# Expert results scattered by token into zeroed DRAM rows and read back by plain transfers, in a mixture-of-experts tail

## The chip, the cores and the metric

The kernel runs on one core of one Trainium2 chip, as one program. The metric is the device time of an execution in microseconds. Before the change it was 1543.15 us, the median of three runs (1536.94, 1543.15 and 1543.61).

## The reference

Two blocks stand behind each other on 512 tokens of width 1024. The first (gated linear attention, a state-space layer and a feed-forward net) and the attention and convolution of the second come before the change; the change is in the second block's mixture of experts. Cut to what matters:

```
def hierarchical_moe(h, ...):                  # t: (512, 1024), 4 groups of 8 experts, D_EXPERT 128
    g_val, g_idx = top_k(softmax(t @ rg_w + rg_b), 1)
    e_val, e_idx = top_k(softmax(logits of the chosen group), 2)     # two experts a token
    combine = one_hot(group) * g_val * w_group
    out += einsum('tef,efd->td', silu(t @ e_gate) * (t @ e_up) * combine, e_down)
x = x + gt2 * hierarchical_moe(...)
return rmsnorm_2(x, final_norm_g)
```

Each token goes to two experts, so 1024 expert rows of 1024 numbers have to come back to 512 tokens and be added to `x`, before the norm over each row that ends the kernel.

## The kernel before

The expert stage handles the 32 experts two at a time, in 16 steps (j = 0 to 15, called expert steps here). A step has 128 slots, 64 for each of its experts; about 64 of the 128 are filled, as 1024 rows go to 16 steps. `route` and `slots` make, for each slot, the number of the token that it holds (`idx` for the gathers, `tok` for one-hot matrices), past the bound where the slot is empty.

A step does this. `expert_rows` (L1763), an indirect gather issued by POOL, brings the tokens' rows from `h_dram` to SBUF, three steps ahead. `expert_in` transposes them on PE (L1774) and evacuates them half on ACT, half on DVE (`xT`). `expert_up` multiplies with the gate and up weights (L1793), and ACT and DVE form the activation (L1795 to L1797). `expert_turn` transposes it (L1804), `expert_down` multiplies with the down weights (L1816), and DVE scales the rows by the combine weight (L1817) into `y`, one of three buffers (`ys`; in the trace `ey` and the two halves of a `wd` tile). SP loads the weights, 3 MB a step, into six slots (`wslots`), and each load waits until PE has done with the slot.

Steps 0 to 13 (`SPREAD` is 14) store `y` to `y_dram` from SP, 128 rows at the place j*128 (`down`, L2337). Steps 14 and 15 go another way: `split_rows` halves the f32 rows into two parts that PE multiplies with one-hot matrices (`spread_mm`, L1839), and `spread_add` (L1845) adds the sums from PSUM to `x2`, the residual in SBUF. After step 13's store, `gather_back` (L1861) runs eight indirect gathers on POOL, two for each of the four tiles of 128 tokens, that add rows of `y_dram` to `x2` while they land; `route_back` made their row numbers. `final_out` then norms each of the four tiles (ACT sum of squares L1874, POOL L1876, DVE L125 to L129 and L1881, ACT L1882) and stores it (L1884).

The program's order is not the written one: a list scheduler with a simulated timeline sets it, and `issue_after` and `behind` put single instructions behind others. Each engine then works its own list off in order, so an instruction that waits holds up all behind it on its engine; a transfer's issue is such an instruction on SP or POOL. In that list the weight loads stand behind `e.last_load`, which `down` set to its store.

Earlier, the feed-forward net of the first block runs beside `ada_part` (L855), which loads `ada_w_2` in 48 pieces of 512 KB from POOL (L862) for DVE to sum (L866).

Of the kernel before, what the change touches and what calls it, by code (L numbers as in the profile page):

```python
# [20 lines left out]
SEQ = 512  # L21
# [1671 lines left out]

def route_back(e, pool, T):

    V = e.nc.vector
    first, past = T("r0", 2, 4), T("rp", 2, 4)
    V.tensor_mul(e.scr, e.ohf, e.efirst[:, None, None, :].to_broadcast([128, 2, 4, 32]))
    V.reduce_sum(first, e.scr, axis=mybir.AxisListType.X)
    V.tensor_scalar(past, e.rank, 64.0, OUT, op0=OP.is_ge, op1=OP.mult)  # L1700
    V.tensor_add(past, past, e.rank)
    V.tensor_add(first, first, past)
    e.back = pool.tile([128, 2, 4], I32, name="back")
    V.tensor_copy(e.back, first)


def slot_sums(e, oh, place):
# [10 lines left out]
def slots(e, pool, oh, rnd=None):  # L1718

    V = e.nc.vector  # L1720
    rk = e.rank
    if rnd is not None:
        rk = pool.tile([128, 2, 4], F32, name="srk")
        V.scalar_tensor_tensor(rk, rnd.to_broadcast([128, 8]).rearrange("p (a t) -> p a t", a=2), -64.0, e.rank,
                               op0=OP.mult, op1=OP.add)
    V.tensor_tensor(oh, rk.rearrange("p a t -> p (a t)")[:, :, None].to_broadcast([128, 8, 64]),
                    e.cnt[:, None, :].to_broadcast([128, 8, 64]), op=OP.is_equal)
    p = slot_sums(e, oh, e.place16).rearrange("p (x v) -> p x v", v=2)
    idx = pool.tile([128, 16], I32, name="sidx")
    col = pool.tile([128, 16], F32, name="scol")  # L1730
    V.tensor_copy(col, p[:, :, 0])
    add = lambda out, c: V.scalar_tensor_tensor(out, col, float(c), p[:, :, 1], op0=OP.add, op1=OP.add)
    add(idx, 2 * SEQ)
    tok = pool.tile([128, 16, 4], F32, name="stok")
    for t in range(4):
        last = add(tok[:, :, t], 2 * SEQ - 128 * t)
    e.slots = [last] if rnd is not None else [last, e.placed]
    return idx, tok
# [84 lines left out]
def split_rows(e, y, hl, oh, tok):  # L1823
# [5 lines left out]
    for c in HALVES:  # L1829
        nc.scalar.copy(hl[0][:, c], y[:, c])  # L1830
        V.tensor_sub(hl[1][:, c], y[:, c], hl[0][:, c].bitcast(F32))

# [22 lines left out]

def gather_back(e):

    last = ()
    for t, a in ((0, 0), (1, 0), (2, 0), (0, 1), (3, 0), (1, 1), (2, 1), (3, 1)):
        with behind(e, last):  # L1860
            last = [e.nc.gpsimd.indirect_dma_start(  # L1861
                out=e.x2[:, t], out_offset=None, in_=e.y_dram,
                in_offset=bass.IndirectOffsetOnAxis(ap=e.back[:, a, t:t + 1], axis=0),
                bounds_check=SPREAD * 128 - 1, oob_is_err=False, compute_op=OP.add)]

# [76 lines left out]
def block(ctx, tc, A, out, stop=None, dbg=None):  # L1942
# [44 lines left out]
    for a in range(2):  # L1987
        nc.gpsimd.iota(e.tid[:, 4 * a:4 * a + 4, 1], pattern=[[128, 4]], base=-2 * SEQ, channel_multiplier=0,
                       allow_small_or_imprecise_dtypes=True)
    e.cnt = c.tile([128, 64], F32, name="cnt")  # L1990
    nc.gpsimd.iota(e.cnt, pattern=[[1, 64]], base=0, channel_multiplier=0, allow_small_or_imprecise_dtypes=True)
    e.m2c = c.tile([128, 8], F32, name="m2c")
    e.sh2c = c.tile([128, 8], F32, name="sh2c")
    e.h3_dram = dram("h3_dram", [SEQ, DM])
    e.y_dram = dram("y_dram", [SPREAD * 128, DM])
    e.hg = c.tile([128, 8], F32, name="hg")
# [146 lines left out]
    with P(name="f1", bufs=1, **Lf) as fp:  # L2143
# [4 lines left out]
        V.tensor_scalar(e.ca, e.ca, 0.5, None, op0=OP.mult)  # L2148

        def ada():  # L2150
            for i in range(6):
                yield from ada_part(e, fp, i)

# [111 lines left out]
    T = carve(c[:, 0], c[:, 1])  # L2265
    e.efirst = kp.tile([128, 32], F32, name="efirst")
    nc.gpsimd.iota(e.efirst, pattern=[[64, 32]], base=0, channel_multiplier=0, allow_small_or_imprecise_dtypes=True)
    rnd = kp.tile([128, 1], F32, name="rnd")
# [53 lines left out]
    with P(name="mo", bufs=1, **Lf) as mp:  # L2322
# [4 lines left out]
        def split(j):  # L2327
            split_rows(e, ys[j % 3], hl[j % 2], ohs[j % 2], tok0[:, j])

        def down(j):  # L2330
# [3 lines left out]
            if late and j > 10:  # L2334
                split(j)
            elif not late:
                e.last_load = nc.sync.dma_start(e.y_dram[j * 128:j * 128 + 128], y)  # L2337

        pieces = [p for j in range(n, 16) for p in expert_pieces(e, j, wslots[j % n])]
        early = pieces.pop(2)  # L2340
# [10 lines left out]
        for j in range(17):  # L2351
            if j - 2 in groups:
                spread(e, hl, ohs)
            if j == BACK + 1:
                gather_back(e)
            if 0 < j < 15:
# [5 lines left out]
            if j == 15:  # L2362
                down(j - 1)
                spread14(range(EARLY14))
            if j < 16:
                up = expert_up(e, j, xT[j % 2], wslots[j % n][0])
            if j == 0:
                with behind(e, (up,)):
                    expert_in(e, xT[1], xgs[1])
                route_back(e, kp, T)  # L2370
                nc.sync.dma_start(*early)
# [7 lines left out]
            if j == 11:  # L2379
# [8 lines left out]
                for i in range(SPREAD, 11):  # L2388
                    split(i)
    with P(name="co", bufs=1, **Lf) as cp:  # L2390
        nc.scalar.activation(cp.tile([128, 1], F32, name="warm"), e.eps, AF.Sqrt)
# [127 lines left out]
```

## Time and profile before

| | us |
|---|---|
| median of three runs | 1543.15 (1536.94 to 1543.61) |
| the profiled execution | 1536.67 |
| its span | 1534.9 |
| PE busy | 1449.8 (94%) |
| DVE busy | 886.0 (58%) |
| ACT busy | 656.2 (43%) |
| POOL busy | 534.2 (35%) |

The span runs from the first to the last instruction that the profiler saw, and the execution's time is 1.8 us longer. A busy share is a mean over all stages. What a change in the last stage is worth is read there: in the windows from 1380 us on, in the chain that ended last, and in the rows of the engines whose work it moves.

### The profile page before, as it was taken

Reading aid. Unit: us, or ns where it says so; the run is one execution under the profiler, and the core shown is the slowest. Engines: PE = TensorE matmul, PEld = TensorE weight load, DVE = VectorE, ACT = ScalarE, POOL = GpSimd, SP = SyncE. Lnnn points to the kernel's source line nnn. Section 1 sums busy time; section 2 is a strip of 40 time slices with the busy share of each in tenths; the row PEclk is TensorE's granted clock in tenths of the full one; section 3 lists DMA queues with packets and bytes.
Section 4 is the critical chain, followed back from the end, with each engine's and each line's share of the span. In section 5 each row is a group of like instructions: output and inputs, shape, how many; then the busy total and the mean of one; then the engine's idle time right before and its main releaser. Section 6 shows DMA issues by size and latency. Waiting matters only on the chain. (4 is left out here: it accounts for less than half of the span.)

```text
span 1534.9 us, 23800 instructions
## 1 busy us (share of the span) xinstructions
PE 1449.8 (94%) x9408; PEld 1230.7 (80%) x9408; DVE 886.0 (58%) x1532; ACT 656.2 (43%) x1081; POOL 534.2 (35%) x594
## 2 busy tenths in 40 slices
PE   7999999899999999999999999899999999988994
PEld 7999998677888899897997979898777777975542
DVE  6586644445244566645536454855788776544544
ACT  6564332645322333323223133447767773443323
POOL 0356888222001121412213022508777714112104
PEclk9999999999999999999999999899999999988997
DMA  5842222458463352554545343411221336868997
GB/s 208 190 92 97 90 87 100 115 168 263 150 230 107 114 192 83 192 193 163 194 137 176 125 166 138 144 64 52 93 72 63 106 119 221 344 267 293 411 406 177
DMA packets 73947, 253.49 MB, mean 165 GB/s; under 512 B 20912, under 2 KB 25792, under 8 KB 57188
## 3 DMA queue, kind: packets, MB, share of 16 engines
q1 hardware_dynamic: 38256, 180.18, 32.8%
q0 software_dynamic: 16192, 49.54, 11.6%
q10 hardware_dynamic: 19380, 22.17, 4.5%
q8 instruction: 76, 1.25, 0.3%
q14 instruction: 43, 0.35, 0.1%
HBM read 226.65 MB, written 32.17 MB: 169 GB/s over the span
## 5 line engine op out<-in xcount | busy, mean ns | idle before, releaser
L74 DVE TENSOR_TENSOR wlo<-raw,whi 128x2048 fp32r<-128x2048 f32 x73 | 177.7, 2434 | 125.0 <-ACT whi L73 125.0
L73 ACT CAST whi<-raw 128x2048 fp32r<-128x2048 f32 x76 | 145.2, 1911 | 184.2 <-PE ps L98 94.5
L1117 POOL TENSOR_TENSOR uc<-uc,u 128x512 f32<-128x512 f32 x77 | 114.7, 1490 | 75.7 <-ACT u L1114 69.2
L98 PE MATMUL ps<-wlo,hh 128*128 128x256 f32 x416 | 117.1, 283 | 2.5 <-DVE wlo L74 2.5
L97 PE MATMUL ps<-xhi,whi 128*128 128x264 f32 (+1 forms) x352 | 119.0, 340 | 0.0
L98 PE MATMUL ps<-xlo,whi 128*128 128x264 f32 (+1 forms) x352 | 117.9, 335 | 0.3 <-DVE xlo L1930 0.3
L99 PE MATMUL ps<-xhi,wlo 128*128 128x264 f32 (+1 forms) x352 | 117.5, 334 | 0.0
L97 PE MATMUL ps<-whi,hh 128*128 128x256 f32 x416 | 116.8, 283 | 0.0
L99 PE MATMUL ps<-whi,hl 128*128 128x256 f32 x416 | 116.5, 281 | 0.0
L99 PE MATMUL ps<-hn,wlo 128*128 128x512 f32 (+1 forms) x256 | 97.6, 382 | 0.0
L98 PE MATMUL ps<-hn,whi 128*128 128x512 f32 (+1 forms) x256 | 97.6, 382 | 0.0
L97 PE MATMUL ps<-hn,whi 128*128 128x512 f32 (+1 forms) x256 | 97.5, 383 | 0.0
L905 POOL TENSOR_TENSOR fr<-fr 128x512 f32<-128x512 f32 x32 | 52.6, 1643 | 110.7 <-ACT fr L904 110.4
L866 DVE SCALAR_TENSOR_TENSOR aacc<-araw,ca,aacc 128x1024 f32<-128x1024 f32 x42 | 55.7, 1326 | 46.3 <-DMA araw<-in_ada_w_dram 46.0
L98 PEld LDWEIGHTS ps<-wlo,hh 128*128 128x128 f32 x416 | 79.1, 190 | 3.7 <-DVE wlo L74 2.7
L97 PEld LDWEIGHTS ps<-whi,hh 128*128 128x128 f32 x416 | 78.9, 190 | 1.9 <-issue 1.7
L99 PEld LDWEIGHTS ps<-whi,hl 128*128 128x128 f32 x416 | 79.4, 191 | 0.0
L862 POOL DMA_DIRECT2D araw<-in_ada_w_dram x48 | 26.3, 548 | 145.3 <-DVE aacc L866 91.0
L97 PE MATMUL ps<-whi,xhi 128*128 128x256 f32 x256 | 74.9, 293 | 0.0
L99 PE MATMUL ps<-whi,xlo 128*128 128x256 f32 x256 | 74.3, 290 | 0.0
L98 PE MATMUL ps<-wlo,xhi 128*128 128x256 f32 x256 | 73.6, 287 | 0.0
L97 PEld LDWEIGHTS ps<-xhi,whi 128*128 128x128 f32 x352 | 65.9, 188 | 8.9 <-issue 2.2
(675 smaller groups left out, 4214.3 us busy)
## 6 DMA issues: line engine op xcount, KB each, us to landing
raw<-in_w_ff_dram SPq DMA_DIRECT2D x32, 1024.0 KB
wg<-in_w_eg_dram SPq DMA_DIRECT2D x26, 1024.0 KB
araw<-in_ada_w_dram POOLq DMA_DIRECT2D x48, 512.0 KB, 4.6
wd<-in_w_ed_dram SPq DMA_DIRECT2D x10, 1024.0 KB
raw<-in_w_glu_dram SPq DMA_DIRECT2D x8, 1024.0 KB
wse<-in_w_eg_dram SPq DMA_DIRECT2D x6, 1024.0 KB
y_dram<-wd SPq DMA_DIRECT2D x9, 512.0 KB
U<-u_dram POOLq DMA_DIRECT2D x16, 264.0 KB, 3.7
```

What stands on the lines that cost most here:

```text
L73: nc.scalar.copy(hi[:, :n], raw[:, :n])
L74: sub.tensor_sub(lo[:, :n], raw[:, :n], hi[:, :n])
L97: nc.tensor.matmul(out, lhsT=ah, rhs=bh, start=(first and i == 0), stop=False)
L98: nc.tensor.matmul(out, lhsT=ah, rhs=bl, start=False, stop=False)
L99: nc.tensor.matmul(out, lhsT=al, rhs=bh, start=False, stop=(last and i == n - 1))
L862: nc.gpsimd.dma_start(raw, A["ada_w_2"][k * 128:(k + 1) * 128, i * DM:(i + 1) * DM])
L866: V.scalar_tensor_tensor(acc, raw, e.ca[:, k:k + 1], acc, op0=OP.mult, op1=OP.add)
L905: nc.gpsimd.tensor_mul(r, r, r)
L1117: nc.gpsimd.tensor_add(y, y, tmp)
```

## The change

The results of steps 0 to 13 are no longer stored by slot. `slots` also makes `e.to`, for each slot the row a*512 + token, where a is 0 or 1 for a token's first or second expert (the one-hot sums carry 128 more for the second, from `e.tid`; `second` splits it off again), and past the bound where the slot is empty. `down` scatters `y` by these numbers into `y_dram`, now 1024 rows, with an indirect transfer issued by POOL. Rows whose expert is in steps 14 and 15 stay zero: four transfers of zeros from POOL, 1 MB each, fill the tensor during the feed-forward net. After step 13, `rows_back` loads the eight blocks of 128 rows with plain transfers from SP into weight slots that are free by then (slot 5 and half of slot 0; in the trace they bear names like `wg` and `wd`). DVE adds four of them to `x2` (tokens 0 to 255), POOL three, DVE the last one. `route_back` and `gather_back` go. `e.last_load` is no longer set in `down`.

```diff
 def slots(e, pool, oh, rnd=None):
-    V.tensor_copy(col, p[:, :, 0])
+    second = pool.tile([128, 16], F32, name="ssec")
+    V.tensor_scalar(second, p[:, :, 0], 127.5, -128.0, op0=OP.is_ge, op1=OP.mult)
+    V.tensor_add(col, p[:, :, 0], second)
...
+    if rnd is None:
+        V.scalar_tensor_tensor(second, second, -4.0, col, op0=OP.mult, op1=OP.add)
+        e.to = pool.tile([128, 16], I32, name="sto")
+        V.scalar_tensor_tensor(e.to, second, float(2 * SEQ), p[:, :, 1], op0=OP.add, op1=OP.add)
...
-def gather_back(e):
-
-    last = ()
-    for t, a in ((0, 0), (1, 0), (2, 0), (0, 1), (3, 0), (1, 1), (2, 1), (3, 1)):
-        with behind(e, last):
-            last = [e.nc.gpsimd.indirect_dma_start(
-                out=e.x2[:, t], out_offset=None, in_=e.y_dram,
-                in_offset=bass.IndirectOffsetOnAxis(ap=e.back[:, a, t:t + 1], axis=0),
-                bounds_check=SPREAD * 128 - 1, oob_is_err=False, compute_op=OP.add)]
+def rows_back(e, views):
+
+    for t in range(4):
+        for a in range(2):
+            e.nc.sync.dma_start(views[2 * t + a], e.y_dram[a * SEQ + t * 128:a * SEQ + t * 128 + 128])
...
+    V.tensor_scalar(e.tid[:, 4:8, 0], e.tid[:, 4:8, 0], 128.0, None, op0=OP.add)
...
-    e.y_dram = dram("y_dram", [SPREAD * 128, DM])
+    e.y_dram = dram("y_dram", [2 * SEQ, DM])
...
+        zero = fp.tile([128, DM], F32, name="zero")
+        nc.gpsimd.memset(zero, 0.0)
         def ada():
             for i in range(6):
+                if i < 4:
+                    nc.gpsimd.dma_start(e.y_dram[256 * i:256 * i + 256].rearrange("(p r) d -> p r d", r=2),
+                                        zero[:, None, :].to_broadcast([128, 2, DM]))
                 yield from ada_part(e, fp, i)
...
         def down(j):
             if late and j > 10:
-                split(j)
+                e.halves = split(j)
             elif not late:
-                e.last_load = nc.sync.dma_start(e.y_dram[j * 128:j * 128 + 128], y)
+                nc.gpsimd.indirect_dma_start(out=e.y_dram, out_offset=bass.IndirectOffsetOnAxis(ap=e.to[:, j:j + 1], axis=0),
+                                             in_=y, in_offset=None, bounds_check=2 * SEQ - 1, oob_is_err=False)
...
             if j == BACK + 1:
-                gather_back(e)
+                rows_back(e, yb)
...
             if j == 15:
                 down(j - 1)
+                with behind(e, (e.halves,)):
+                    for t in range(2):
+                        for a in range(2):
+                            V.tensor_add(e.x2[:, t], e.x2[:, t], yb[2 * t + a])
+                for y in (4, 5, 6):
+                    nc.gpsimd.tensor_add(e.x2[:, y // 2], e.x2[:, y // 2], yb[y])
                 spread14(range(EARLY14))
...
+        with behind(e, (e.halves,)):
+            V.tensor_add(e.x2[:, 3], e.x2[:, 3], yb[7])
```

What this does to POOL's list. In the rows, `h` is the buffer of an expert gather and `sidx` its row numbers; `x2t` is the residual `x2`; `sto` is `e.to`. A wait on `DMASW` with a number is for the landing of an earlier transfer issued by POOL (their semaphores are taken in turn, 0 to 7), one on `PE` or `DVE` for that engine. Before, the last four expert gathers are followed by the gathers back:

```order
L1763 DMA h_12545<-h_dram,sidx 128x1024 [waits DMASW4_49,PE_49]
L1763 DMA h_12545<-h_dram,sidx 128x1024 [waits DMASW5_49,PE_49]
L1763 DMA h_12546<-h_dram,sidx 128x1024 [waits DMASW6_49,PE_49]
L1763 DMA h_12546<-h_dram,sidx 128x1024 [waits DMASW7_49,PE_49]
L1861 DMA x2t<-y_dram,back 128x1024 [waits DMAHW4_49,DMAHW3_49,DMAHW5_49,DMAHW2_49,DMAHW6_49,DMAHW1_49,DMAHW7_49,DMAHW0_49,DVE_49]
L1861 DMA x2t<-y_dram,back 128x1024 x2
L1861 DMA x2t<-y_dram,back 128x1024 [waits DMASW4_49]
L1861 DMA x2t<-y_dram,back 128x1024 [waits DMASW0_49]
L1861 DMA x2t<-y_dram,back 128x1024 [waits DMASW5_49,DMASW1_49]
L1861 DMA x2t<-y_dram,back 128x1024 [waits DMASW6_49,DMASW2_49]
```


Now, the last five expert gathers (steps 11 to 15) and scatters 3 to 9:

```order
L1756 DMA h_12553<-h_dram,sidx 128x1024 [waits DMASW0_49,PE_49]
L1756 DMA h_12552<-h_dram,sidx 128x1024 [waits DMASW1_49,PE_49]
L1756 DMA h_12552<-h_dram,sidx 128x1024 [waits DMASW3_49,PE_49]
L2332 DMA y_dram<-ey,sto 1024x1024 [waits DMASW5_49,DVE_49]
L1756 DMA h_12553<-h_dram,sidx 128x1024 [waits DMASW4_49,PE_49]
L1756 DMA h_12553<-h_dram,sidx 128x1024 [waits DMASW6_49,PE_49]
L2332 DMA y_dram<-wd_9927,sto 1024x1024 [waits DMASW1_49,DVE_49]
L2332 DMA y_dram<-wd_9927,sto 1024x1024 [waits DMASW4_49,DVE_49]
L2332 DMA y_dram<-ey,sto 1024x1024 [waits DMASW5_49,DVE_49]
L2332 DMA y_dram<-wd_9927,sto 1024x1024 [waits DMASW7_49,DMASW6_49,DVE_49]
L2332 DMA y_dram<-wd_9927,sto 1024x1024 [waits DMASW7_49,DMASW0_49,DVE_49]
L2332 DMA y_dram<-ey,sto 1024x1024 [waits DMASW0_49,DVE_49]
```


The eight gathers back at the list's end are gone, and fourteen scatters are in it, three of them above this piece and four below. Counted in turn, scatter 3 holds semaphore 1, scatters 4 to 7 hold 4 to 7 and scatters 8 and 9 hold 0 and 1; so each scatter waits, besides DVE's rows, for the landing of the one before it. Scatter 3 stands behind the gather for step 13, scatter 4 behind the one for step 15.

On DVE, the end of the expert stage. `hl` are the halves that `split_rows` makes, `tri` is the buffer of step 15's activation, `ps` PSUM. Before, from the halves of step 14 to the first sum:

```order
L1831 TENSOR_TENSOR hl_15023<-wd_9920,hl_15022 128x512 [waits DMAHW3_49,Activation_49]
L1831 TENSOR_TENSOR hl_15023<-wd_9920,hl_15022 128x512 [waits Activation_49]
L1796 SCALAR_TENSOR_TENSOR tri<-tri,ps 128x128 [waits Activation_49]
L1797 TENSOR_TENSOR tri<-tri,ps 128x128 [waits DVE_49]
L1817 SCALAR_TENSOR_TENSOR ey<-ps,swt,gt_12586 128x512 [waits DMAHW2_49,PE_49]
L1817 SCALAR_TENSOR_TENSOR ey<-ps,swt,gt_12586 128x512 [waits PE_49]
L1831 TENSOR_TENSOR hl_15025<-ey,hl_15024 128x512 [waits Activation_49] x2
L1845 TENSOR_TENSOR x2t<-x2t,ps 128x512 [waits DMASW7_49,PE_49]
L1845 TENSOR_TENSOR x2t<-x2t,ps 128x512 [waits PE_49]
```


Now the same stretch, cut off at step 15's own halves:

```order
L1824 TENSOR_TENSOR hl_15050<-wd_9927,hl_15049 128x512 [waits DMAHW6_49,DMAHW5_49,Activation_49]
L1824 TENSOR_TENSOR hl_15050<-wd_9927,hl_15049 128x512 [waits Activation_49]
L2366 TENSOR_TENSOR x2t<-x2t,wg_12405 128x1024 [waits DMAHW1_49,DMAHW0_49]
L2366 TENSOR_TENSOR x2t<-x2t,wg_12405 128x1024 [waits DMAHW2_49,DVE_49]
L2366 TENSOR_TENSOR x2t<-x2t,wg_12582 128x1024 [waits DMAHW3_49]
L1789 SCALAR_TENSOR_TENSOR tri<-tri,ps 128x128 [waits Activation_49]
L2366 TENSOR_TENSOR x2t<-x2t,wg_12582 128x1024 [waits DMAHW4_49,DVE_49]
L1790 TENSOR_TENSOR tri<-tri,ps 128x128 [waits DVE_49]
L1810 SCALAR_TENSOR_TENSOR ey<-ps,swt,gt_12591 128x512 [waits DMASW4_49,PE_49]
L1824 TENSOR_TENSOR hl_15052<-ey,hl_15051 128x512 [waits Activation_49]
```


Four additions of read-back rows (L2366) have come between step 14's halves and the two operations of step 15's activation (L1789 and L1790, before L1796 and L1797), and each waits for a plain load.

## Rows read from the trace of the kernel before

**Rows 1.** of the page: GB/s moved in the 40 slices of the span

```profile
GB/s 208 190 92 97 90 87 100 115 168 263 150 230 107 114 192 83 192 193 163 194 137 176 125 166 138 144 64 52 93 72 63 106 119 221 344 267 293 411 406 177
```

**Rows 2.** busy time by ten-microsecond windows of the expert stage, all engines

```profile
core 0: us, PE busy (x) PEld busy (x) DVE busy (x) ACT busy (x) POOL busy (x), PEclk, DMA share, GB/s
1390.00:1400.00 10.00, 10.00 (x78) 7.32 (x79) 4.63 (x14) 4.97 (x14) 3.11 (x4) 0.84 0.86 284
...
1450.00:1460.00 10.00, 10.00 (x82) 6.19 (x82) 5.73 (x13) 3.94 (x11) 1.98 (x2) 1.00 1.02 422
...
1480.00:1490.00 10.00, 9.12 (x55) 4.79 (x56) 2.87 (x7) 2.20 (x7) 0.00 (x0) 1.00 1.01 417
...
1520.00:1530.00 10.00, 0.00 (x0) 0.00 (x0) 9.29 (x27) 6.37 (x14) 3.84 (x3) 0.50 0.54 153
```

**Rows 3.** chain of waits, last part: start us, duration us, what

```profile
1392.37 4.00 PE ps L1793 x32
...
1412.04 3.60 PE ps L1793 x32
...
1418.49 3.60 PE ps L1793 x32
...
1472.40 0.33 PE ps L1804
...
1480.88 0.33 PE ps L1804
...
1493.44 6.05 DMA y_dram<-wd
...
1506.48 0.20 issue
1506.68 8.64 DMA x2t<-y_dram,back
...
1518.28 6.11 DMA x2t<-y_dram,back
```

**Rows 4.** DMA from 1380 us: packets, MB, share; issues with us to landing

```profile
q0 software_dynamic: 3600, 8.31, 21.7%
...
h<-h_dram,sidx POOLq DMA_INDIRECT x16, 9.1
...
x2t<-y_dram,back POOLq DMA_INDIRECT x8, 8.1
```

**Rows 5.** expert gathers (L1763), 1440 to 1465 us, then all: landings in us

```profile
DMA to landing us min/median/max: 9.3/9.3/10.2
...
DMA to landing us min/median/max: 3.9/9.1/10.2
```

**Rows 6.** timeline: start us, us, engine line op out<-in

```profile
1457.38 0.99 POOL L1763 DMA_INDIRECT h<-h_dram,sidx  x1 [5.46 <-PE ps L1804]
...
1508.14 0.29 DVE L1797 TENSOR_TENSOR tri<-tri,ps 128x128 f32<-128x128 f32 x1
...
1511.11 5.74 PE L1839 MATMUL ps<-hl,oh 128*128 128x512 f32 x24
...
1520.41 0.15 DVE L127 TENSOR_TENSOR rsa<-rsa 128x1 f32<-128x1 f32 x1
...
1520.57 1.27 POOL L1876 TENSOR_TENSOR fg<-x2t,gf 128x512 f32<-128x512 f32 x1 [0.72 <-DVE rsa L127]
1520.59 1.26 DVE L128 SCALAR_TENSOR_TENSOR rsa<-rsa 128x1 f32<-128x1 f32 x1
...
1524.48 1.28 DVE L1845 TENSOR_TENSOR x2t<-x2t,ps 128x512 f32<-128x512 f32 x2 [0.57 <-DMA x2t<-y_dram,back]
```

**Rows 7.** of the page: costliest groups, DVE over 128x1024

```profile
L866 DVE SCALAR_TENSOR_TENSOR aacc<-araw,ca,aacc 128x1024 f32<-128x1024 f32 x42 | 55.7, 1326 | 46.3 <-DMA araw<-in_ada_w_dram 46.0
```

**Rows 8.** ada_w loads (L862), all: landing; then a window there, columns as rows 2

```profile
DMA to landing us min/median/max: 3.7/4.6/8.0
...
600.00:640.00 40.00, 38.66 (x247) 34.58 (x247) 28.87 (x30) 15.45 (x23) 15.55 (x18) 1.00 0.60 199
```

More of the change, by code (lines that the diff above doesn't have):

```diff
@@ L1691, in route_weights @@
     V.tensor_mul(e.place.rearrange("p (a t) x -> p a t x", a=2), e.ohf, comb[:, :, :, None].to_broadcast([128, 2, 4, 32]))
[L1694 to L1704, printed above, removed]
 def slot_sums(e, oh, place):
@@ L1830, in split_rows @@
         nc.scalar.copy(hl[0][:, c], y[:, c])
-        V.tensor_sub(hl[1][:, c], y[:, c], hl[0][:, c].bitcast(F32))
+        last = V.tensor_sub(hl[1][:, c], y[:, c], hl[0][:, c].bitcast(F32))
+    return last
 def spread_mm(e, ps, ys, ohs, t, first=True, last=True):
@@ L2265, in block @@
     T = carve(c[:, 0], c[:, 1])
-    e.efirst = kp.tile([128, 32], F32, name="efirst")
-    nc.gpsimd.iota(e.efirst, pattern=[[64, 32]], base=0, channel_multiplier=0, allow_small_or_imprecise_dtypes=True)
     rnd = kp.tile([128, 1], F32, name="rnd")
@@ L2327, in split @@
         def split(j):
-            split_rows(e, ys[j % 3], hl[j % 2], ohs[j % 2], tok0[:, j])
+            return split_rows(e, ys[j % 3], hl[j % 2], ohs[j % 2], tok0[:, j])
         def down(j):
@@ L2334, in down @@
             if late and j > 10:
-                split(j)
+                e.halves = split(j)
             elif not late:
-                e.last_load = nc.sync.dma_start(e.y_dram[j * 128:j * 128 + 128], y)
+                nc.gpsimd.indirect_dma_start(out=e.y_dram, out_offset=bass.IndirectOffsetOnAxis(ap=e.to[:, j:j + 1], axis=0),
+                                             in_=y, in_offset=None, bounds_check=2 * SEQ - 1, oob_is_err=False)
+        flat = lambda w: w.rearrange("p k c -> p (k c)")
+        yb = [v[:, c:c + 1024] for v in (flat(wslots[5][0][0]), flat(wslots[5][0][1]), flat(wslots[5][1]),
+                                         flat(first[0].rearrange("p g k c -> p (g k) c"))) for c in (0, 1024)]
         pieces = [p for j in range(n, 16) for p in expert_pieces(e, j, wslots[j % n])]
@@ L2369, in block @@
                     expert_in(e, xT[1], xgs[1])
-                route_back(e, kp, T)
                 nc.sync.dma_start(*early)
```

## The prediction

> **What bounds the kernel now.** I read the slices of the page first: the last quarter of the span is where the change acts, and the two fullest DMA slices of the whole kernel lie there, 411 and 406 GB/s [rows 1]. The ten-microsecond windows show why: in those from 1450 and 1480 us the DMA engines are at a share of 1.0, 422 and 417 GB/s, while PE is busy 10.0 and 9.1 of 10 us; from 1520 PE does nothing [rows 2]. So the stage is held by PE and transfers together, and its tail by something else. The chain names that: the last store of expert rows takes 6.05 us, then two accumulating gathers stand in the chain with 8.64 and 6.11 us [rows 3]. PE has ended at 1516.85 (1511.11 + 5.74 [rows 6]); the last gather lands at 1524.4 (1518.28 + 6.11). The span ends at 1534.9. That 7.5 us is what the change can reach in the tail at most, plus what fewer bytes in the stage give.
>
> **What it removes.** Fourteen plain stores of 512 KB on SP, 7.3 MB, and eight accumulating gathers that land 8.1 us after issue in the median [rows 4]. In the window from 1380 us on POOL's queue moves only 8.31 MB for 16 gathers, 8 gathers back and half a down weight [rows 4]; 24 full gathers would be 12.6 MB, so rows past the bound are not moved. The scatters likewise move only the filled slots, about 64 of 128 rows, 0.25 MB each: 3.6 MB instead of 7.3. The 3.7 MB less are, at 420 GB/s, some 8.8 us of a full DMA stage, so I put the end of the saturated stretch at 1482 instead of 1490.
>
> **What it adds, at the head.** Four stores of zeros (4.2 MB, 10 us at 420 GB/s) go into POOL's queue at the start of the feed-forward stage, ahead of most of the `ada_w` loads. There DMA is at 0.60 and PE at 38.7 of 40 us [rows 8]: hidden, cost 0. If the cover failed it would be those 10 us once. One more small DVE operation lies on the way to the slot numbers: 0.15 us like the 128x1 operation of [rows 6]; I count 0.2. The six small operations of `route_back` go from DVE beside PE work: 0.
>
> **What it adds, in the stage: a serial chain.** This is the term that decides. All fourteen scatters write one DRAM tile, and the order shows that each waits on the completion semaphore of the one before, on POOL, in order. Before, the stores stood on SP and waited only for their data. So a scatter cannot start until the last has landed, and its period is landing plus hand-over.
>
> Price of a landing: no scatter stands in the trace. The nearest row is the expert gather: same instruction form, same queue, same slots, so the same bytes. It takes 0.99 us of POOL, and from issue to landing 9.3 us in the saturated stretch, 3.9 us at the least before it is saturated [rows 5]. The hand-over is 0.2 us ("issue" of 0.20 us before the 1506.68 gather [rows 3]). So 9.5 us under load and 4.1 us free; for a store into DRAM I take 4.5 free, near the gather's 4.1 and under the 6.05 of the plain store of twice the bytes [rows 3]. Bounds: 4.1 throughout from below, 9.5 throughout from above.
>
> The Trainium skill, "DMA: Bandwidth & Descriptors", section on the anatomy of one DMA by the GpSimd path, gives about 2.0 us plus bytes over 436 GB/s per transfer, and says that the receipt of a write is heaviest in HBM. For 0.25 MB that is an estimate of 2.6 us, and with 0.2 of hand-over the chain's ten periods would be 28 us. The gather rows at 9.3 us under load do not agree with it; it has no term for other queues' traffic.
>
> Start of the chain: in POOL's new order the fifth scatter stands behind the last expert gather, which goes out when PE has transposed expert step 11, at 1457.38 [rows 6]. PE's order up to there is the same as before. So scatter 4 goes at 1458.4. From there ten landings follow (scatters 4 to 13) with nothing else in between: two at 9.5 (to 1477), one that sees the load end, 7.5, and seven at 4.5: 58 us. The last lands at T = 1516.5.
>
> What hangs behind on the other engines: with three buffers for expert rows, DVE's row scaling of step k waits for scatter k-3, and DVE runs in order, so the activations of steps 12 to 14 wait with it and PE stands idle for some 20 us. Worked along, the scaling of step 13 comes at about 1511, 2 us before its scatter's turn at 1512: the scatters stay the longer path.
>
> **From T to the end.** SP's eight reads wait for the last scatter. The first lands 3.7 to 4.6 us after issue (the `ada_w` loads, same 512 KB [rows 8]), say T + 4.5 with the wait; each further one 1.26 us later (512 KB at 416 GB/s). On DVE three of the additions, 1.3 us each for 128x1024 f32 [rows 7], stand ahead of step 15's activation, a fourth in the middle of it (the row is the nearest of that size): that is through at T + 10. From there to PE's end it was 8.4 us (1508.43 to 1516.85 [rows 6]): T + 18.4. PE comes from a pause, and after the pause before the stage the granted clock was 0.84 of 2.4 GHz, a mean over stretches at that level and at 1.2, and the first 32 products took 4.00 us instead of 3.60 [rows 2, 3]: I add 1. POOL's three additions begin when the fifth read has landed, T + 9.5, at twice 1.27 us each (128x512 [rows 6]): T + 17.5. During a POOL addition a DVE operation of one column took 1.26 us instead of 0.15 [rows 6], so the halves' subtractions and DVE's last addition follow at about T + 19. Then six spread additions (0.65 each), the first norms, two more: T + 26. From the last spread addition to the end it is 9.1 us as before (1525.76 to 1534.9). Sum: T + 35 = 1551.5.
>
> The wait of 1.26 us speaks against the split of the additions between DVE and POOL: both kinds read two tensors in SBUF. The Trainium skill, "SBUF — State Buffer", section "Who interferes with whom", says that a DVE instruction with two SBUF inputs and a GpSimd instruction that reads SBUF block each other for the whole instruction; by that rule, and the trace agrees with 1.26 us, the two share nothing while both run. Without it the sum would be about 2 us less.
>
> **Sum.** Span 1551.5 + 0.2 against 1534.9, so 16.8 us more. The profiled execution took 1536.67, 1.8 above its span: 1553.5. The median shown is 1543.15, 6.5 above that execution, which stands with the lowest of the three runs (1536.94). I forecast 1555, a little toward the median.
>
> **Rivals.**
> A, the scatters keep pace. If a scatter lands in 3 us even under load, ten periods are 32, T = 1490, and PE's even rhythm sets it: 6.45 us a step (1412.04 to 1418.49 [rows 3]) instead of the 8.5 between the transposes of steps 11 and 12 [rows 3] (the new PE order holds the plain sequence to the end, and the bytes fall). Then T + 35, 1525, plus 1.8 and 0.2: 1527, faster. It decides below a mean period of 3.4. The estimate of 2.6 us, from the Trainium skill's page "DMA: Bandwidth & Descriptors", would give this. For it: the fall of bytes. Against it: 9.3 us for the same bytes on the same queue [rows 5]. 6 in 100.
> B, even. Free landings nearly throughout, mean 4.2 to 4.8: T = 1500 to 1506, end 1537 to 1543. For it: 3.9 us at the least. Against it: at 1458 the DMA share is 1.0 and stays there for two or three scatters whatever happens [rows 2]. 12 in 100.
> C, the chain as summed, mean period 5 to 7: 1545 to 1568. 66 in 100.
> D, longer landings. If stores by row into DRAM need 7 us free, or the saturated stretch lasts as long as before, the chain is 70 to 95 us: 1566 to 1590. For it: the 6.05 us store. Against: half the bytes. 14 in 100.
> E, the waits do not bind because the order changes nothing on the chip, the read-back alone counts: the reads wait for scatter 13 at 1494, T = 1499 by a 4.5 us landing, 1536. 2 in 100, even.
>
> **Numbers.** Likeliest C, own range 1545 to 1568. With a piece of B and D outside, 8 in 10 is 1538 to 1572. Half a per cent (about what a measurement of this kernel tells from no change) is 7.7 us, that is T before 1492 or after 1508 against the profiled execution. Faster 0.07, same 0.13, slower 0.80.
>
> **What would show it.** In the new trace: POOL's idle time before the scatters ended by the scatter before (y_dram), some 50 us from 1458 on; landings near 9 us up to about 1480 and 4 to 5 after; DVE's row scaling waiting for a DMA; PE idle in 1475 to 1530; first read after 1510; step 15's activation behind three additions; POOL's additions lengthening DVE operations. Wrong if scatters land in under 4 us while the weights stream, or if PE's busy share from 1460 to 1500 stays at 8 of 10 or more. Then the end would be set by rival A's rhythm, and the time would be under 1540.

## The result and the profile after

The changed kernel takes 1554.3 us, the median of five runs (1550.97 to 1557.57), beside 1542.95 for the kernel before: ratio 1.008, 95% interval 1.0058 to 1.0102, so 9 to 16 us more. Run again, beside further runs of the kernel before, it is 1.0092 (1.0077 to 1.0108). The profiled execution is the slowest of the five, 1557.57 us with a span of 1555.7.

The page's GB/s of the 40 slices, to be held against [rows 1]: the last two full slices, the 38th and 39th before (411 and 406), are now the 37th and 38th (373 and 417), and the 39th, from 1478 us on, moves 174.

```profile
GB/s 210 187 88 97 86 86 99 120 172 255 151 217 109 125 173 116 274 180 176 189 124 190 128 179 128 116 75 65 85 71 72 85 222 178 399 186 373 417 174 170
```

The ten-microsecond windows of the changed kernel, columns as in [rows 2]:

```profile
1470.00:1480.00 10.00, 8.02 (x53) 3.89 (x53) 3.36 (x8) 2.34 (x6) 0.99 (x1) 1.00 1.02 418
1480.00:1490.00 10.00, 5.72 (x29) 3.24 (x31) 5.84 (x16) 2.00 (x5) 0.97 (x1) 0.74 0.95 394
1490.00:1500.00 10.00, 5.18 (x32) 2.61 (x28) 2.41 (x4) 1.17 (x3) 1.28 (x2) 0.84 0.24 97
1500.00:1510.00 10.00, 9.02 (x45) 4.46 (x45) 5.71 (x13) 1.62 (x5) 2.78 (x4) 0.74 0.16 56
```

From 1480 to 1500 us PE works little over half the time, the granted clock falls below 1, and from 1490 on the DMA engines do almost nothing either (0.24). Nothing is short there: something waits. The timeline of POOL says what. Columns: start us, us, engine, line, operation, and in brackets the idle time before it and what ended it. L1756 is the expert gather, L2332 the scatter of a step's rows:

```profile
1463.47 1.00 POOL L1756 DMA_INDIRECT h<-h_dram,sidx  x1 [5.44 <-PE ps L1767]
1464.78 1.02 POOL L2332 DMA_INDIRECT y_dram<-wd,sto  x1 [0.30 <-DVE xT L1771]
1476.09 0.99 POOL L2332 DMA_INDIRECT y_dram<-wd,sto  x1 [10.30 <-DMA y_dram<-wd,sto]
1485.33 0.97 POOL L2332 DMA_INDIRECT y_dram<-ey,sto  x1 [8.25 <-DMA y_dram<-wd,sto]
1494.02 0.97 POOL L2332 DMA_INDIRECT y_dram<-wd,sto  x1 [7.72 <-issue]
1499.68 0.97 POOL L2332 DMA_INDIRECT y_dram<-wd,sto  x1 [4.70 <-DMA y_dram<-wd,sto]
1503.03 0.97 POOL L2332 DMA_INDIRECT y_dram<-ey,sto  x1 [2.38 <-DMA y_dram<-wd,sto]
...
1513.21 0.97 POOL L2332 DMA_INDIRECT y_dram<-ey,sto  x1 [2.43 <-DVE xT L1771]
1518.09 0.97 POOL L2332 DMA_INDIRECT y_dram<-wd,sto  x1 [3.91 <-DVE wd L1810]
```

These are scatters 4 to 9, 12 and 13. Each idle time before scatters 5 to 12 ends 0.74 to 0.78 us behind the landing of the scatter before (where another releaser is named, that one had long been done), and the periods fall from 11.3 to 3.4 us as the weights end. The last one waits for DVE instead. Landings of the scatters issued from 1380 to 1482 us and from there on, then of all sixteen expert gathers (before: [rows 5]):

```profile
DMA to landing us min/median/max: 8.5/10.1/11.3
...
DMA to landing us min/median/max: 2.6/2.9/7.9
...
DMA to landing us min/median/max: 4.0/8.6/12.1
```

The last part of the chain of waits, where [rows 3] ended in two accumulating gathers: scatter 7 and its landing, the scaling of step 10 on DVE (its buffer is the one that scatter 7 empties), the products of step 13 (1501.46) and of step 14, the scaling of step 13 on DVE, the last scatter, two reads on SP, the landing of a read, then DVE.

```profile
1494.02 4.89 DMA y_dram<-wd,sto
...
1499.00 1.41 DVE wd L1810 x2
...
1501.46 5.48 PE ps L1786 x32
...
1511.69 3.60 PE ps L1786 x32
1515.30 1.74 PE ps L1809 x8
1517.06 0.76 DVE wd L1810
1517.82 0.27 issue
1518.09 3.20 DMA y_dram<-wd,sto
...
1522.19 6.14 DMA wg<-y_dram
```

The last scatter lands at 1521.3 us (1518.09 + 3.20), which is the prediction's T; from there to the end of the span it is 34.4 us. Before, the last store landed at 1499.49 (1493.44 + 6.05 [rows 3]), 35.4 us ahead of the end. The tail is 1.0 us shorter. What the change costs lies ahead of T. From scatter 7's landing at 1498.9 us on, the chain does not run through scatters 8 to 12 but through DVE and PE; what that means for the prediction is said below.

A first look misleads in one point: the two profiled executions differ by 20.8 us of span, and 6.1 of it is there when the last expert gather goes out (1463.47 against 1457.38 [rows 6]), some 4 us of it already at the first load of `ada_w_2` (613.9 us against 609.2, less 0.9 us in which POOL clears the buffer of zeros). So the traces are compared from that gather on.

| us | before | after | after, again |
|---|---|---|---|
| last expert gather to T (before: last store landed) | 42.1 | 57.8 | 57.1 |
| T to the end of the span | 35.4 | 34.4 | 33.7 |
| sum | 77.5 | 92.2 | 90.8 |

The change adds 13.3 to 14.7 us from the gather on, in line with the ratios (0.8 to 0.92% of 1543 is 12.3 to 14.2 us).

### The profile page after: what moved, and what is told of

Same layout as the page of the kernel before. It is cut to its first block, busy times and chain, and to the rows that moved or that the text cites. A ratio compares the mean times of both kernels' runs of the same rounds, so it can differ in the third digit from the quotient of the medians.

```text
span 1555.7 us, 23817 instructions
## 1 busy us (share of the span) xinstructions
PE 1457.2 (94%) x9408; PEld 1234.2 (79%) x9408; DVE 893.8 (57%) x1535; ACT 655.3 (42%) x1081; POOL 546.0 (35%) x607
## 5 line engine op out<-in xcount | busy, mean ns | idle before, releaser
L866 DVE SCALAR_TENSOR_TENSOR aacc<-araw,ca,aacc 128x1024 f32<-128x1024 f32 x42 | 60.0, 1428 | 41.9 <-DMA araw<-in_ada_w_dram 41.4
L862 POOL DMA_DIRECT2D araw<-in_ada_w_dram x48 | 26.2, 546 | 145.1 <-DVE aacc L866 86.5
```

Of the source, the lines that this page charges most:

```text
L862: nc.gpsimd.dma_start(raw, A["ada_w_2"][k * 128:(k + 1) * 128, i * DM:(i + 1) * DM])
L866: V.scalar_tensor_tensor(acc, raw, e.ca[:, k:k + 1], acc, op0=OP.mult, op1=OP.add)
```

## The experiments

**The changed kernel again.** Nothing is edited; it stands beside the experiments on the tail.

> The changed kernel as it is, on the same chip and beside the same runs of the kernel before, as the measure for the two edits of its tail: ratio to the kernel before 1.006 to 1.011. If the late start of its expert stage in the first profile (5.9 us) is chance between executions, that stage starts here within 4 us of where it starts in the profile of the kernel before, and the tail is as long as there; if it belongs to the change, it is again 5 to 7 us late.

Ratio 1.0092 (1.0077 to 1.0108), median 1551.93. Its first expert gather goes out at 1382.4 us, in the first profile of the changed kernel at 1390.2, in the kernel before at 1384.3: the late start does not belong to the change. POOL's timeline in this execution, same columns, scatters 4, 5, 12 and 13:

```profile
1457.12 1.02 POOL L2332 DMA_INDIRECT y_dram<-wd,sto  x1 [0.30 <-DVE xT L1771]
1468.52 0.99 POOL L2332 DMA_INDIRECT y_dram<-wd,sto  x1 [10.38 <-DMA y_dram<-wd,sto]
...
1504.00 0.97 POOL L2332 DMA_INDIRECT y_dram<-ey,sto  x1 [2.44 <-DVE xT L1771]
1509.72 0.97 POOL L2332 DMA_INDIRECT y_dram<-wd,sto  x1 [4.75 <-DVE wd L1810]
```

The chain is the same within a microsecond when it starts 7.7 us sooner: from scatter 4 to T it takes 55.8 us (T is 1512.9, 1509.72 and a landing of 3.20), in the first profile 56.5.

**A DRAM tensor for each scatter.** This takes the waits between scatters away and no instruction; the reads bring back the rows of step 13 alone.

```diff
-    e.y_dram = dram("y_dram", [2 * SEQ, DM])
+    e.y_drams = [dram(f"yd{i}", [2 * SEQ, DM]) for i in range(SPREAD)]
+    e.y_dram = e.y_drams[SPREAD - 1]
...
-                nc.gpsimd.indirect_dma_start(out=e.y_dram, out_offset=bass.IndirectOffsetOnAxis(ap=e.to[:, j:j + 1], axis=0),
+                nc.gpsimd.indirect_dma_start(out=e.y_drams[j], out_offset=bass.IndirectOffsetOnAxis(ap=e.to[:, j:j + 1], axis=0),
```

> The changed kernel, but each of the fourteen scatters writes a DRAM tensor of its own, so that none waits for the one before; the reads wait for the scatter of step 13 alone, and the rows of steps 0 to 12 are left out of the output. Instructions and bytes are otherwise the same. Theory (the scatters wait for each other, and that chain sets step 13): each scatter goes out when its rows are ready, PE keeps its rhythm, the last scatter lands at 1495 to 1505 us of the span instead of 1521, the end is 16 to 25 us earlier than in the changed kernel, ratio to the kernel before 0.985 to 0.997. Rival (the scatters themselves and the reading back cost it, the waits are covered by other work): the last scatter lands within 4 us of 1521, and the time is the changed kernel's, ratio 1.005 to 1.01.

Ratio 0.9997 (0.9984 to 1.001), median 1537.44. The profile's waits of this kernel, from 1400 to 1500 us (engine and line, what it waited for: us, times, longest), and then, from its chain, the last scatter:

```profile
POOL yd L2333 <- DVE wd L1810: 36.5, 8, 7.0
POOL yd L2333 <- DVE ey L1810: 27.5, 5, 13.7
```

```profile
1495.50 0.76 DVE wd L1810
1496.26 0.27 issue
1496.53 3.20 DMA yd<-wd,sto
```

Every scatter now waits for its rows and none for another scatter, though their landings under load are as long as ever (7.8 to 11.1 us up to 1482). T is 1499.7, the end 1533.6. The thirteen other scatters have landed by 1494.8 us, 5 us before the first read, so that the reads wait for none of them changes nothing here. Between 1.0092 and 0.9997 are 0.95%, 14.6 us (12.8 from the 1.008 of the first measurement): this one edit takes the whole loss away. The rival of the scatters and the reading back as the cost falls; what is left, gathers and stores exchanged for scatters, reads and additions, comes out even with the kernel before. The ratio is a little over the range that I had put down (0.985 to 0.997), since the kernel that loses nothing is no faster than the old one.

**No weights.** The changed kernel, chain and all, with the DMA engines free.

```diff
         early = pieces.pop(2)
+        pieces = []
```

> The changed kernel with the weights of expert steps 7 to 15 left out (what the buffers hold from steps before is used again, so the output is another); all scatters, reads and additions stay. Theory (the landing of a scatter is long because the weights fill the DMA engines, and the chain binds only through that): scatters land in 2.6 to 4 us from the first to the last, the chain keeps pace with PE, the last one lands at 1490 us or sooner, and the end is 25 us or more earlier than in the changed kernel, ratio at most 0.99. Rival (a landing by row is long whatever else is moved): landings of 8 to 11 us up to scatter 7 as in the changed kernel, last one within 5 us of 1521.

Ratio 0.9968 (0.9958 to 0.9978). First the waits from 1380 to 1500 us, then the landings of all fourteen scatters:

```profile
POOL y_dram L2332 <- DVE wd L1810: 44.5, 9, 7.4
```

```profile
DMA to landing us min/median/max: 2.6/3.3/3.8
```

No landing is over 3.8 us, none of the waits for the scatter before is left, and PE runs at 6.45 us a step as in [rows 3]. T is 1493.1, the end 1527.5. So the chain binds only by the length of its links, and their length comes from the weights. The expected size was too large: T came at 1493 and not by 1490, because PE's rhythm is the floor, and against the changed kernel it is 1.2% (19 us), not 25. The run takes away waits for weights too, so its total is no measure of the chain alone; that is the run above.

**The zeros alone, in the kernel before.**

```diff
+    e.z_dram = dram("z_dram", [2 * SEQ, DM])
...
+        zero = fp.tile([128, DM], F32, name="zero")
+        nc.gpsimd.memset(zero, 0.0)
...
+                if i < 4:
+                    nc.gpsimd.dma_start(e.z_dram[256 * i:256 * i + 256].rearrange("(p r) d -> p r d", r=2),
+                                        zero[:, None, :].to_broadcast([128, 2, DM]))
                 yield from ada_part(e, fp, i)
```

> The kernel before, with the 4.2 MB of zeros stored at the same place as in the changed kernel into a DRAM tensor that nothing reads. Prediction (hidden beside the feed-forward stage): no difference, ratio 0.998 to 1.002. Rival (the profile of the changed kernel, whose expert stage begins 5.9 us later, shows the cost of the zeros): 4 to 6 us more, ratio 1.0025 to 1.004; if only the stretch of the feed-forward stage is lengthened, 1.5 to 2 us, ratio 1.001.

Ratio 0.9998 (0.9985 to 1.0012): hidden, as predicted. The `ada_w` additions beside it do get longer, as in the changed kernel: 1385 ns in the mean with the zeros alone, 1428 in the changed kernel, 1326 before [rows 7]. The row of the page, the zeros alone:

```profile
L866 DVE SCALAR_TENSOR_TENSOR aacc<-araw,ca,aacc 128x1024 f32<-128x1024 f32 x42 | 58.2, 1385 | 42.8 <-DMA araw<-in_ada_w_dram 42.1
```

DVE has idle time there (42.8 us ahead of these additions), and the time of the kernel does not rise.

**All additions on DVE.** The three that POOL makes, given to DVE.

```diff
-                    nc.gpsimd.tensor_add(e.x2[:, y // 2], e.x2[:, y // 2], yb[y])
+                    with behind(e, (e.halves,)):
+                        V.tensor_add(e.x2[:, y // 2], e.x2[:, y // 2], yb[y])
```

> The changed kernel with the three additions that stand on POOL moved to DVE, behind the fourth of DVE's own. T is the landing of the last scatter (1521.3 us in the changed kernel), the end there is T + 34.4. Theory (POOL's additions of 2.4 to 2.8 us set the end, since DVE's last addition and the spread additions begin when they are through, at T + 17.2, and they lengthen DVE's operations while they run): three additions of 1.22 us on DVE replace 7.6 us on POOL, the end is T + 31 to T + 33, the time 1 to 3 us under the changed kernel's. Rival (DVE is what the tail is short of, and three more additions on it cost their 3.7 us): the end is T + 36 to T + 38, 2 to 4 us over the changed kernel.

Ratio 1.0085 (1.0071 to 1.01), against 1.0092 for the changed kernel: neither theory's size. T is 1513.4, the end T + 33.8, as in the changed kernel (33.7 and 34.4). The rival's loss of 2 to 4 us is out; the intervals overlap, so a gain of a microsecond or two stays open. In this profile DVE's last addition begins at T + 17.2, in the changed kernel at T + 17.7 and 17.1: the additions that POOL no longer makes stand on DVE among the scalings and halves of step 15 instead.

**DVE's additions behind step 15's rows.**

```diff
                 down(j - 1)
-                with behind(e, (e.halves,)):
-                    for t in range(2):
-                        for a in range(2):
-                            V.tensor_add(e.x2[:, t], e.x2[:, t], yb[2 * t + a])
...
         with behind(e, (e.halves,)):
-            V.tensor_add(e.x2[:, 3], e.x2[:, 3], yb[7])
+            for y in (0, 1, 2, 3, 7):
+                V.tensor_add(e.x2[:, y // 2], e.x2[:, y // 2], yb[y])
```

> The changed kernel with the four additions that DVE does ahead of and within step 15's activation placed behind the rows of step 15 instead, so that PE's path to its end waits for no read; POOL's three stay. Theory (the reads hold the activation of step 15 and by that PE's end): step 15's activation is through some 7 us sooner, PE ends 5 us or more sooner, the end is T + 30 to T + 32.5, the time 2 to 4 us under the changed kernel's. Rival (the additions on both engines and the spread additions set the end, wherever they stand): the end stays at T + 33.5 to T + 36, the time within 1 us of the changed kernel's.

Ratio 1.0123 (1.0108 to 1.0137), slower than the changed kernel by 0.31%, 5 us: both expectations missed. From the first read to the end it is 39.4 us (1515.8 to 1555.2), in the changed kernel 34.4 and 33.7. The timeline of DVE, the last part of step 15's activation, its rows, their lower halves (L1824), and three of the additions (L2392), then POOL's additions:

```profile
1522.47 0.29 DVE L1790 TENSOR_TENSOR tri<-tri,ps 128x128 f32<-128x128 f32 x1
1524.76 1.61 DVE L1810 SCALAR_TENSOR_TENSOR ey<-ps,swt,gt 128x512 f32<-128x512 f32 x2 [2.00 <-PE ps L1809]
1526.28 4.04 DVE L1824 TENSOR_TENSOR hl<-ey,hl 128x512 fp32r<-128x512 f32 x2
1530.24 5.65 DVE L2392 TENSOR_TENSOR x2t<-x2t,wg 128x1024 f32<-128x1024 f32 x3
...
1524.61 5.16 POOL L2364 TENSOR_TENSOR x2t<-x2t,wd 128x1024 f32<-128x1024 f32 x2 [11.11 <-DMA wd<-y_dram]
1529.73 2.81 POOL L2364 TENSOR_TENSOR x2t<-x2t,wg 128x1024 f32<-128x1024 f32 x1
```

The activation is through 7.0 us behind the first read, in the changed kernel 9.8 (1531.12 against 1521.34): the additions held it by 3 us, not 7, since PE's products of step 15 end only at 1521.8. In exchange the additions, which had stood in DVE's waiting time, now stand in the tail. POOL's additions, which run from 1524.6 to 1532.5, lengthen what DVE does beside them: the two subtractions of the halves take 4.04 us, where the two of step 14 took 1.46 with POOL idle. The second of them takes 2.84 us and ends 0.55 us behind POOL's second addition, and the first DVE addition takes 3.38 us and ends 1.1 us behind POOL's third. The Trainium skill, "SBUF — State Buffer", section "Who interferes with whom", says that a DVE instruction with two SBUF inputs contends with a GpSimd instruction that reads SBUF, and calls the shared ports an exclusive lock. These rows agree with it.

**The kernel before with plain gathers** into freed weight buffers, and eight additions on DVE; stores by slot as they were.

```diff
-                out=e.x2[:, t], out_offset=None, in_=e.y_dram,
+                out=views[2 * t + a], out_offset=None, in_=e.y_dram,
...
-                bounds_check=SPREAD * 128 - 1, oob_is_err=False, compute_op=OP.add)]
+                bounds_check=SPREAD * 128, oob_is_err=False)
...
+                for y in range(8):
+                    V.tensor_add(e.x2[:, y // 2], e.x2[:, y // 2], yb[y])
```

> The kernel before, with its stores by slot on SP, but with the eight accumulating gathers replaced by eight plain gathers into freed weight buffers, which need not wait for one another, and eight additions on DVE; assignments past the bound point at a row of zeros behind the slots. Theory (what the kernel before loses at its end is the chain of gathers that wait for one another, and the changed kernel pays for the same gain with the chain of scatters): PE's rhythm up to step 13 is as before, all gathers have landed some 15 us after the last store, the last additions end 3 to 6 us earlier, and the time is 2 to 6 us under the kernel before, ratio 0.996 to 0.999. Rival (the additions stand in DVE's way before step 15, or the gathers land no sooner than the accumulating ones): the same or up to 5 us more, ratio 1.0 to 1.003.

Ratio 1.0037 (1.0024 to 1.005): the rival's sign, a little over its range, and by neither of its two ways. The gathers are issued from 1502.9 to 1513.0 us and land in 6.1 us in the median (before: 8.1 [rows 4]). But the timeline of DVE has its first addition behind step 15's activation, which waits for PE, and the last as late as this:

```profile
1513.18 0.29 DVE L1798 TENSOR_TENSOR tri<-tri,ps 128x128 f32<-128x128 f32 x1
1513.39 1.22 DVE L2372 TENSOR_TENSOR x2t<-x2t,wg 128x1024 f32<-128x1024 f32 x1
...
1526.19 2.30 DVE L2372 TENSOR_TENSOR x2t<-x2t,wd 128x1024 f32<-128x1024 f32 x1
1528.55 1.20 DVE L2372 TENSOR_TENSOR x2t<-x2t,wg 128x1024 f32<-128x1024 f32 x1
```

These are the eight additions of 1.2 us and more that the accumulating transfers had made without DVE; five of them start after 1520 us, behind step 15's rows. So the gathers land sooner and nothing stands ahead of step 15; the additions cost their time in the tail.

**The last gather ahead of the first norm,** in the kernel before.

```diff
+    e.gathered = last
...
-    nc.gpsimd.tensor_mul(g, e.x2[:, t, HALVES[1]], gf[:, HALVES[1]])
+    with behind(e, e.gathered):
+        nc.gpsimd.tensor_mul(g, e.x2[:, t, HALVES[1]], gf[:, HALVES[1]])
```

> The kernel before with one edit in its tail: POOL's first multiplication of the final norm, which stands there between the seventh and the eighth accumulating gather, is put behind the eighth. In the kernel before it runs at 1516.84 to 1518.14 us of the span and waited 2.06 us for DVE, and the last gather goes out at 1518.28, though the gather that it must wait for has landed at 1515.4. Theory (the last gather ends the chain): it goes out near 1515.4, lands at 1521.5, and the time falls by 2 to 3 us, ratio 0.998 to 0.9987. Rival (the norms of the first tile are held instead, and give it back): within 1 us, ratio 0.9993 to 1.0007.

Ratio 1.0004 (0.9992 to 1.0016): no gain, in the rival's range. The last gather and its landing, from the chain:

```profile
1524.40 7.64 DMA x2t<-y_dram,back
```

It goes out 16.6 us behind the first gather (1507.79) instead of 17.9 (1500.43 to 1518.28), but takes 7.64 us to land instead of 6.11 [rows 3]. The expectation had read the wrong landing: the last gather adds to the same tile as the fifth, and waits for that one. In the kernel before the fifth lands at 1516.7 us (1508.52 and 8.17), and not at 1515.4, near which the fourth lands (1515.3); so of the 2.9 us that were to be gained at most 1.6 were there.

**Half of the gathers plain,** in the kernel before: what the runs above suggest, additions only where DVE waits.

```diff
+                added = [V.tensor_add(e.x2[:, t], e.x2[:, t], yb[t]) for t in range(2)]
...
+                with behind(e, added):
+                    up = expert_up(e, j, xT[j % 2], wslots[j % n][0])
...
+                for t in range(2, 4):
+                    V.tensor_add(e.x2[:, t], e.x2[:, t], yb[t])
+                gather_back(e, yb, 1)
```

> The kernel before with its stores by slot, and of its eight accumulating gathers only four left: the other four (one for each tile of tokens) go first, as plain gathers into two freed weight buffers, and DVE adds them, two ahead of step 15's activation and two within it, where DVE waits for PE in the kernel before (5.87 us ahead of that activation). Theory (additions cost nothing where DVE waits anyway, and four gathers that nothing holds shorten the chain of gathers at the end): the four plain ones land 6 us after issue, the last accumulating one goes out some 13 us after the first gather and lands 19 to 21 us after it, against 24 in the kernel before; the time falls by 2 to 4 us, ratio 0.997 to 0.999. Rival (the additions hold step 15's activation and so PE, or the waits for DVE hold the accumulating gathers): the same or up to 4 us more, ratio 1.0 to 1.003.

Ratio 1.0001 (0.9988 to 1.0014): the rival, at the low end of its range. The last gather goes out 13.1 us behind the first, as expected, and lands 21.5 us behind it (19 to 21 expected), but the chain no longer runs through it:

```profile
1508.17 5.96 DMA wg<-y_dram,back
1514.16 1.23 DVE x2t L2387
1515.38 0.21 DVE tri L1798
...
1516.54 3.68 PE ps L1817 x8
```

The third addition got between the two halves of step 15's activation (L1797 and L1798), and PE is late in place of the gather. From the first gather to the end it is 33.6 us against 34.5, a gain that the interval cannot show. No version here that does all the work beats the kernel before.

## Why the prediction was right

The forecast of 1555 us against 1554.3 is nearer than its working. The change was priced at 16.8 us of span, and the runs show 12 to 15. The rest of the agreement comes from the base: I took the profiled execution (1536.67 us) and added 1.5 toward the median, while the median of the kernel before beside these runs lies 6.3 us above it. That part of the agreement is luck. Sign and place were right, and so was the mechanism up to scatter 7; the size was 2 to 4 us too large.

**The chain decides.** Right, and shown: without the waits between scatters the ratio falls from 1.0092 to 0.9997, and with short landings the waits vanish by themselves.

**Its start.** Scatter 4 a microsecond behind the last expert gather: 1.3 us (1463.47 to 1464.78).

**Its length.** 58 us were predicted from scatter 4 to T; it was 56.5 (1464.78 to 1521.29). The sum hides two errors of opposite sign. With its hand-over of 0.2 us in each period, the prediction took the ten landings as 56.0 us, and they took 48.7; what stands between a landing and the next scatter it took as 2.0 us, and it was 7.8. By part: the three landings under load were taken as 9.3, 9.3 and 7.3 and were 10.5, 8.5 and 7.9, and the load ended about where predicted (the DMA share is 1.00 from 1486 to 1488 us and 0.78 and 0.50 in the next two windows of 2 us; 1488 is 1482 on the time of the kernel before). The seven free landings were taken as 4.3 and were 4.9 once, then 2.6 to 3.2. I had argued from the 6.05 us of the plain store that a store by row needs more than a gather when nothing else moves; it needs less. The hand-over was taken as 0.2 from a piece called "issue" [rows 3]; it is 0.74 to 0.78 at each of scatters 5 to 12, and 1.75 ahead of scatter 13, where the wait for its rows is in it. So the free landing and the hand-over are the terms that were mis-sized, and that they nearly cancel is luck. The estimate of 2.6 us from the Trainium skill's "DMA: Bandwidth & Descriptors", section on the anatomy of one DMA, fits a free scatter (2.6 to 3.2 us here) and is too low by a factor of three to four while the weights stream; rival A, which took 3 us under load too, fell with that.

**The slack before the last scatter.** Here a step failed. The prediction has the scatters as the longer path to scatter 13, with DVE's scaling of step 13 ready 2 us before the scatter's turn (its own two times, 1511 and 1512, are 1 us apart). Scatter 12 landed at 1516.34, so by the hand-over the next could have gone at 1517.1; it went at 1518.09, 1.0 us later, because the rows were late. The longer path was the one through the three buffers: DVE's scalings of steps 9, 10 and 11 waited 6.0, 4.3 and 1.5 us for the landings of scatters 6, 7 and 8, and from step 10's scaling (1499.00 us in the chain) it went on over PE to step 13's. PE had stood still for 5.8 us, and the 32 products of step 13's gate and up weights (1501.46 us in the chain) took 5.48 us instead of 3.60, in a window with a granted clock of 0.74, a mean over times at 1.2 and 2.4 GHz. In the second profile of the changed kernel PE had stood still for 4.1 us, the products took 6.36 and the scatter was 1.8 us late. In both the loss on the products (1.9 and 2.8 us) is more than the delay; that the clock alone makes it was not tried by itself. So from scatter 7 on it is the length of the first, loaded links that counts, and scatters 8 to 12 ran beside the path that decided, 1.0 and 1.8 us shorter than it.

**T to the end.** 35 us predicted, 34.4 and 33.7 measured. The steps stand in the timeline of the changed kernel (DVE and POOL; L2366, L2368 and L2395 are the additions of what was read back):

```profile
1525.16 2.50 DVE L2366 TENSOR_TENSOR x2t<-x2t,wg 128x1024 f32<-128x1024 f32 x2 [3.35 <-DMA wg<-y_dram]
1528.35 1.22 DVE L2366 TENSOR_TENSOR x2t<-x2t,wg 128x1024 f32<-128x1024 f32 x1 [0.69 <-DMA wg<-y_dram]
...
1530.83 0.28 DVE L1790 TENSOR_TENSOR tri<-tri,ps 128x128 f32<-128x128 f32 x1
1530.96 4.78 POOL L2368 TENSOR_TENSOR x2t<-x2t,wd 128x1024 f32<-128x1024 f32 x2 [11.90 <-DMA wd<-y_dram]
...
1535.69 2.84 POOL L2368 TENSOR_TENSOR x2t<-x2t,wg 128x1024 f32<-128x1024 f32 x1
...
1539.01 1.21 DVE L2395 TENSOR_TENSOR x2t<-x2t,wg 128x1024 f32<-128x1024 f32 x1
```

First addition at T + 3.9 (4.5 predicted), activation through at T + 9.8 (10), POOL's additions done at T + 17.2 (17.5) at 2.4 to 2.8 us each, DVE's last begun at T + 17.7 (done by 19). The claim that without DVE and POOL holding each other the sum would be 2 us less is not borne out by the run with all additions on DVE (under 1 us, inside its interval); but that run also gives DVE 3.7 us more to do, so it does not test the claim alone. The row that the prediction calls a POOL addition [rows 6, 1520.57] is a multiplication of the final norm.

**The costs put at nothing.** The zeros are hidden: 0.9998. Of the fewer bytes I made nothing but an earlier end of the load, and the run with a tensor for each scatter shows no gain in the end: even with the chain gone the time is that of the kernel before. What the bytes alone are worth was not measured.

**The rivals.** A and E gave 1527 and 1536 for a kernel whose waits don't bind. The run that has no waits took 1535.68 in its profile, near E's figure; A's T of 1490 asked for PE's even rhythm, which in that run still stops for weights (busy 6.1 of the 10 us from 1470 to 1480 us; the last gather to T took 41.9 us). B and D are out: the mean period was 5.65 us (56.5 over ten), in C's 5 to 7, above B's 4.2 to 4.8 and below D's 7 to 9.5. C's upper bound of 1568 does not follow from its 7 us, which give 1565 (1458.4 + 70, then 35, 1.8 and 0.2).

**What was to be seen.** POOL's idle time before scatters 5 to 12 is 41 us (45 with the wait of scatter 13 for its rows), predicted some 50 over all; PE idles 18 of the 70 us from 1460 to 1530, predicted 20.

## What to carry to other kernels

Look in the program's order whether transfers that write one DRAM tensor by index are put behind each other's landing, as the scatters were here. Then count the links behind the last point where other work covers them, price each link at what that queue shows at that place, loaded and free apart, with the hand-over read from rows too, and follow the buffers that each landing frees: here the path went over to them half-way. Before giving up accumulating transfers for loads and additions, see whether DVE has waiting time where the additions would stand. Four additions there held step 15's activation by 3 us; moved into the tail they made the kernel 5 us slower. Where profiled executions of two kernels differ ahead of the change, line them up at the last common event before subtracting, and take the base from the median.

## What was not expected

Landings by row on POOL's queue depend on the other traffic by a factor of about three: 2.6 to 3.8 us for all fourteen scatters without weights (median 3.3), 8.5 to 11.3 for those issued up to 1482 us with them (median 10.1), for the same 0.25 MB. They are short again as soon as the load ends, within two scatters (8.7, 5.7, then 3.4 us of period).

A scatter of 128 rows is no dearer than a gather: 0.97 to 1.02 us of POOL and 2.6 to 3.2 us to land when free, about half of the 6.05 us of the plain store of all 128 rows at the end of the loaded stretch [rows 3]. A plain gather takes 0.99 us of POOL, an accumulating one 1.54 to 1.61 in the kernel before.

Two executions of the changed kernel differ by 8 us in where the expert stage begins (first gather at 1382.4 and 1390.2 us), with nothing edited; 35 runs of the kernel before span 1533.58 to 1543.73.
